# Gated-delta mixer of a two-layer hybrid network: residual normalised before the split, convolution from PSUM, heads inverted in fours

## The chip, the cores and the metric

The kernel runs on one core of one Trainium2 chip. The metric is the device time of one execution in microseconds (us). An execution consists of a span, in which the engines' instructions lie, and about 3 us around it.

## The reference, cut to what matters

The network has two layers of 1024 tokens by 1024 channels. Each layer is a mixer, a cross-attention to 256 memory tokens and a squared-ReLU MLP; before each of them stands a normalisation, `h = x * y * g`, where `y` is one over the root mean square of a token's channels and `g` a gain per channel. The change lies in the mixer of the second layer, a gated delta network:

```python
def c_mixer(h, w_in, conv_w, a_log, dt_bias, head_gain, w_out):
    qkv, gate, b, a = _split(h @ w_in, C_SIZES)      # 3072, 1024, 8 and 8 channels
    qkv = jax.nn.silu(short_conv(qkv, conv_w))       # four taps along the tokens, per channel
    q, k, v = _split(qkv, (GDN_QK, GDN_QK, GDN_VW))
    q = l2norm(q.reshape(B, T, GDN_HEADS, GDN_DK))   # 8 heads of 128
    k = l2norm(k.reshape(B, T, GDN_HEADS, GDN_DK))
    ...
    o = gated_deltanet(q, k, v, beta, log_alpha)
    o = rmsnorm(o, head_gain) * jax.nn.silu(gate...)
    return o @ w_out

def gated_deltanet(...):                             # chunks of 64 tokens
    lower = jnp.where(strict, beta * (k @ k.T) * decay, 0.0)
    sol = triangular_solve(lower + eye, rhs, ...)    # 64 x 64, for each head and chunk
    def step(S, inp):                                # over the 16 chunks of a head
        v_new = u - wk @ S
        o = qd @ S + att @ v_new
        S = S * jnp.exp(gl) + kd.T @ v_new
```

## The kernel before, in words

**Layout and order.** All of `x` lies transposed in SBUF, as 8 tiles of 128 channels by two halves of 512 tokens. The code runs under a scheduler with a timeline of its own: it decides in which order the instructions stand in each engine's queue, and each queue is then worked off strictly in that order. Instructions within `high_priority` are put ahead of others that are ready.

**Projections.** A projection of 128 output channels by one half of the tokens is 24 matmuls of 128x512 (`mm3`, L156 to L158): 8 blocks of input channels, with weights and `h` both split into a high and a low part (`hi*hi`, `lo*hi`, `hi*lo`). I call it a unit. ACT makes the high part of the weights (L149), POOL the low part (L150). The result lies in one of two PSUM banks of the tile `mm`. In program order the mixer has units 1 to 48 for the heads (six for each head: k, q and v of both halves), 49 to 64 for the output gates, then the memory's keys and values for the cross-attention, then 65 to 80 for the output projection.

**Start.** `mix_start` (L350) splits `x * g` into `hh` (ACT, L240) and `hl` (DVE, L241), 8 tiles for each half. The factor `y` isn't in it. Since it is a factor per token, it is multiplied on the result: `scaled` (L431, DVE) reads the bank, multiplies by the row `yy` and writes `raw` in SBUF. So the units can run before `y` is known.

**A head.** `gdn_head` (L958) projects k, q and v, with `scaled` as the eviction of each. `gdn_pre` (L987) then makes the convolution from `raw`: one ACT multiplication (L1002) and three DVE multiply-adds (L1004), a tanh (L1007, ACT) and a product (L1008, DVE), which together are the SiLU. It transposes (L1014, L1071), makes sums of squares (L1022) and the products of keys and queries (L1050), and multiplies them by decays `M`. `M` is loaded by a DMA from `gr` (L1037) and has one buffer; ACT makes `qe` of it (L1039). The triangles go through DRAM (`Ud`, `Bd`).

**Inversion.** `gdn_inv` (L1093) takes two heads at a time. It loads the 32x32 diagonal blocks of the triangles onto 64 partitions, solves them in 31 steps of two DVE instructions (L1109, L1114), stores them in `Xd`, loads the result as full tiles, transposes (L1124) and makes the 64x64 and 128x128 inverses of each head from five groups of 8 matmuls (L1129, L1136, L1140) with a subtraction or copy behind each group.

**Recurrence.** `gdn_rec` (L1145) walks over the 16 chunks of 2 heads, or at the end of 4, with `rec` matmuls (L1171 to L1191), each behind a DVE step (L1172, L1177, L1185). The order in the code is: heads 0 and 1, their inversion, their recurrence; the same for 2 and 3; heads 4 and 5 with inversion; heads 6 and 7 with inversion; the recurrence of heads 4 to 7.

**Gates.** `c_gate` (L871) projects, evicts with `scaled`, takes the tanh (L881) and the product (L882), and multiplies with the recurrence's output (`od`, L885).

Of the kernel before, what the change touches and what calls it, by code (L numbers as in the profile page):

```python
# [26 lines left out]
class Model:  # L27
# [216 lines left out]

    def split(self, vec, stat):
# [104 lines left out]
    def mix_start(self, l, bank, right):  # L350

        self.stat_bank = bank
        self.split(l, lambda half: self.y0 if l == 1 and half == 0 else self.rms_rows(half))
        self.flush()
        self.stat_bank = "sc"
        self.x_src = self.a["xT"]
        if l == 1:
            self.x_src = self.dr.tile([NK, 128, 1024], F32, name="x_scratch")
        self.x_close(self.x_src if l == 1 else None)
        self.open_right(right)  # L360
        self.direct = {}
        self.od = [self.dr.tile([128, 1024], F32, tag=f"od{l}{i}", name=self.nm("od")) for i in range(8)]

    def mix(self, l):
# [10 lines left out]
        else:  # L375
            with self.phase(
# [4 lines left out]
                self.mix_start(l, "o", dict(raw=5, kq=2, vc=1, M=1, qe=1, ua=1, kv=2))  # L381
# [437 lines left out]
    def mix_c(self):  # L819
# [4 lines left out]
        for pair in ((0, 1), (2, 3), (4, 5), (6, 7)):  # L824
            oq += [self.gdn_head(h) for h in pair]
            if pair[1] == 7:
                self.close_right()
                self.x_open(self.x_src, (0,))
                self.open_right(dict(B2=3, y2=3, S2=4))
            self.gdn_inv(pair)  # L830
            if pair[1] < 4:
                self.gdn_rec(pair, oq)
# [38 lines left out]
    def c_gate(self, h):  # L871
# [3 lines left out]
        def gate(i, w, half):  # L875
# [14 lines left out]
    def c_gates(self):  # L890
# [14 lines left out]
        for half in HALVES:  # L905
# [6 lines left out]
            self.scaled(rows[:32], ps[:32], half)  # L912
            nc.scalar.activation(rows[:32], rows[:32], AF.Identity, bias=bias)
# [44 lines left out]
    def gdn_head(self, h):  # L958

        nc = self.nc  # L960
        raw = {}

        def take(i, w, half):
            t = self.ph2("raw", [128, 515])
            ps = self.proj(w, half)
            with self.tc.high_priority():
                self.scaled(t[:, 3:515], ps, half)
                if half == 0:
                    nc.gpsimd.memset(t[:, 0:3], 0.0)
                else:  # L970
                    nc.gpsimd.tensor_copy(t[:, 0:3], raw[i, 0][:, 512:515])
            raw[i, half] = t
# [6 lines left out]
        for half in HALVES:  # L979
            self.gdn_pre(h, half, [raw[i, half] for i in (8 + h, h, 16 + h)], oq)  # L980
# [6 lines left out]
    def gdn_pre(self, h, half, raws, oq):  # L987
# [9 lines left out]
        kq = self.ph2("kq", [128, 2, 512])  # L997
        vc = self.keep("vc", dt=F32)
        for tl, raw, dst in zip((8 + h, h, 16 + h), raws, (kq[:, 0], kq[:, 1], vc)):
            cv = self.tmp()  # L1000
            wj = lambda j: self.convw[:, tl * 4 + j : tl * 4 + j + 1]
# [5 lines left out]
            nc.scalar.activation(dst, cv, AF.Tanh, scale=0.5)  # L1007
            nc.vector.scalar_tensor_tensor(out=dst, in0=dst, scalar=1.0, in1=cv, op0=ALU.add, op1=ALU.mult)  # L1008
# [762 lines left out]
```

## Time and profile before

| | us |
|---|---|
| three runs | 3225.93, 3229.2, 3229.65 (median 3229.2) |
| profiled execution | 3224.76 |
| its span | 3221.8 |
| PE (TensorE) busy | 3045.2 (95%) |
| DVE (VectorE) busy | 2115.9 (66%) |
| ACT (ScalarE) busy | 1330.2 (41%) |
| POOL (GpSimd) busy | 945.4 (29%) |

The second mixer lies between about 1495 and 2313 us of the span, from its first unit to the end of its output projection. A row of the timeline names the start and the length in us, the engine, the line, the operation, output and inputs; in brackets stands how long the engine was idle before it, and what it waited for. [...]

### The profile page before, as it was taken

How to read it: one execution, taken by the hardware profiler on the slowest of the kernel's cores; microseconds unless marked ns; L12 is line 12 of the kernel's file. 1: busy time of each engine (PE TensorE's matmuls, PEld its weight loads, DVE VectorE, ACT ScalarE, POOL GpSimd, SP SyncE). 2: the span in 40 equal slices, each digit the busy share in tenths (PEclk: the TensorE clock that was granted, in tenths of full speed). 3: DMA queues.
4: the chain of work that ended last, by engine and by line, in shares of the span. 5: the costliest groups of instructions: out<-in, count | busy, mean ns of one | idle time of the engine just before them, and what ended most of it. 6: DMA issues, size and time to landing. Idle time of an engine off the chain costs nothing.

```text
span 3221.8 us, 39997 instructions
## 1 busy us (share of the span) xinstructions
PE 3045.2 (95%) x14447; PEld 2511.5 (78%) x14447; DVE 2115.9 (66%) x3342; ACT 1330.2 (41%) x2525; POOL 945.4 (29%) x725
## 2 busy tenths in 40 slices
PE   8999989999899999998988899899999899999997
PEld 6777777888678878887777788788888678878886
DVE  5567475545786667777777775654454786667777
ACT  3254464424354454433443333234333354444442
POOL 2354565313000032234343333125323100023323
PEclk9999989999899999999999899999999999999998
DMA  4333553213244464443345556665212234474432
GB/s 151 109 119 103 156 175 119 70 39 102 75 143 157 152 238 167 147 164 100 87 117 142 149 156 187 191 231 187 66 56 77 97 111 149 157 250 173 148 144 79
DMA packets 268374, 438.04 MB, mean 136 GB/s; under 512 B 38064, under 2 KB 146832, under 8 KB 261008
## 3 DMA queue, kind: packets, MB, share of 16 engines
q1 hardware_dynamic: 268176, 435.50, 41.4%
q8 instruction: 113, 1.85, 0.2%
q14 instruction: 85, 0.70, 0.1%
HBM read 300.60 MB, written 134.81 MB: 135 GB/s over the span
## 4 chain that ended last, share of the span: by engine, by line
PE 33%; DVE 9%; DMA 4%; issue 4%; POOL 1%; ACT 1%; SPq 0%; POOLq 0%; DVEq 0%; ACTq 0%
PE mm L158 3%; PE mm L157 3%; PE mm L156 3%; PE ga L1453 2%; PE ga L1454 2%; PE ga L1455 2%; PE gb L1454 1%; DVE t L1004 1%; PE gb L1455 1%; PE gb L1453 1%; PE gc L1454 1%; PE gc L1455 1%; PE gc L1453 1%; PE mm L1454 1%; PE mm L1455 1%
## 5 line engine op out<-in xcount | busy, mean ns | idle before, releaser
L156 PE MATMUL mm<-hh,wh 128*128 128x512 f32 x1248 | 503.4, 404 | 8.2 <-DVE raw L431 3.5
L157 PE MATMUL mm<-hl,wh 128*128 128x512 f32 x1248 | 504.3, 404 | 0.0
L158 PE MATMUL mm<-hh,wl 128*128 128x512 f32 x1248 | 501.9, 402 | 0.0
L150 POOL TENSOR_TENSOR wl<-wr,wh 128x1024 fp32r<-128x1024 f32 x128 | 320.6, 2506 | 448.8 <-ACT wh L149 423.4
L1445 POOL TENSOR_TENSOR r<-r,r 128x512 f32<-128x512 f32 x64 | 92.0, 1458 | 881.8 <-DVE lo L1412 881.8
L1412 DVE TENSOR_TENSOR lo<-r,hi 128x1024 fp32r<-128x1024 f32 x192 | 252.8, 1317 | 133.1 <-ACT hi L1411 132.3
L1411 ACT CAST hi<-r 128x1024 fp32r<-128x1024 f32 x192 | 201.6, 1051 | 313.7 <-PE mm L1454 126.6
L156 PEld LDWEIGHTS mm<-hh,wh 128*128 128x128 f32 x1248 | 239.4, 192 | 59.2 <-DVE raw L431 4.8
L158 PEld LDWEIGHTS mm<-hh,wl 128*128 128x128 f32 x1248 | 240.5, 193 | 48.3 <-issue 0.9
L157 PEld LDWEIGHTS mm<-hl,wh 128*128 128x128 f32 x1248 | 240.2, 192 | 48.0 <-DVE hl L474 0.4
L149 ACT CAST wh<-wr 128x1024 fp32r<-128x1024 f32 x128 | 133.8, 1046 | 213.2 <-PE mm L157 120.8
L1412 DVE TENSOR_TENSOR lo<-br,hi 128x512 fp32r<-128x512 f32 x224 | 187.0, 852 | 32.9 <-ACT hi L1411 32.8
L1453 PE MATMUL ga<-hi,hi 128*128 128x512 f32 x528 | 206.7, 392 | 1.8 <-ACT w L1550 1.0
L1455 PE MATMUL ga<-hi,lo 128*128 128x512 f32 x528 | 206.5, 391 | 0.0
L1454 PE MATMUL ga<-lo,hi 128*128 128x512 f32 x528 | 206.5, 391 | 0.0
L1411 ACT CAST hi<-br 128x512 fp32r<-128x512 f32 x224 | 133.4, 619 | 152.0 <-PE ga L1455 90.0
L1454 PE MATMUL gb<-lo,hi 128*128 128x512 f32 x432 | 169.8, 393 | 7.6 <-DVE lo L1412 7.6
L1453 PE MATMUL gb<-hi,hi 128*128 128x512 f32 x432 | 169.8, 394 | 3.6 <-ACT hi L1411 3.1
L1454 PE MATMUL gc<-lo,hi 128*128 128x512 f32 x432 | 169.1, 391 | 2.3 <-DVE lo L1412 2.3
L1455 PE MATMUL gb<-hi,lo 128*128 128x512 f32 x432 | 169.0, 392 | 0.0
L1455 PE MATMUL gc<-hi,lo 128*128 128x512 f32 x432 | 168.2, 390 | 0.0
L1453 PE MATMUL gc<-hi,hi 128*128 128x512 f32 x432 | 167.8, 390 | 0.0
(515 smaller groups left out, 7228.5 us busy)
## 6 DMA issues: line engine op xcount, KB each, us to landing
r<-in_w SPq DMA_DIRECT2D x128, 512.0 KB, 4.2
br<-hd SPq DMA_DIRECT2D x56, 1024.0 KB, 5.4
hd<-w SPq DMA_DIRECT2D x160, 256.0 KB, 3.1
B<-Bd SPq DMA_DIRECT2D x64, 384.0 KB, 4.5
hd<-t SPq DMA_DIRECT2D x64, 256.0 KB, 5.2
wr<-in_c_w SPq DMA_DIRECT2D x32, 512.0 KB, 4.3
wr<-in_ab_w SPq DMA_DIRECT2D x24, 512.0 KB, 3.6
pj<-p SPq DMA_DIRECT2D x48, 256.0 KB, 2.1
```

The costliest lines, as they stand in the source:

```text
L149: nc.scalar.copy(hi, raw)
L150: (eng or nc.gpsimd).tensor_sub(lo, raw, hi.bitcast(F32))
L156: mm(out, w[0], x[0], start=first, stop=False)
L157: mm(out, w[0], x[1], start=False, stop=False)
L158: return mm(out, w[1], x[0], start=False, stop=last)
L1004: nc.vector.scalar_tensor_tensor(out=cv, in0=raw[:, j : j + 512], scalar=wj(j), in1=cv, op0=ALU.mult, op1=ALU.add)
L1411: nc.scalar.copy(hi, src)
L1412: (eng or nc.vector).tensor_sub(lo, src, hi.bitcast(F32))
L1445: self.nc.gpsimd.tensor_add(out[:, i : i + 512], a[:, i : i + 512], b[:, i : i + 512])
L1453: mm(ps, hi, b[k][0], start=first and k == 0, stop=False, skip_group_check=True)
L1454: mm(ps, hi, b[k][1], start=False, stop=False, skip_group_check=True)
L1455: mm(ps, lo, b[k][0], start=False, stop=last and k == 3, skip_group_check=True)
```

## The change

The first layer is as before. In the second mixer five things are different:

1. `split_normed` makes `t = x * g * y` (DVE), `hh` (a copy by ACT) and `hl = t - hh` (DVE): two DVE instructions for each tile in place of one. The second half needs its `y` first. `scaled` isn't used in this mixer any more.
2. The convolution reads the bank itself: one ACT multiplication and three DVE multiply-adds on `cv`. The first half's last three columns are kept by a small ACT copy, and the second half has three multiply-adds of one to three columns with them. `raw`, its three-column POOL copies and memsets are gone; `vc` has two buffers.
3. `c_gate` takes tanh and product from the bank.
4. `gdn_inv` takes four heads on 128 partitions: two rounds of the 31 steps in place of four.
5. Heads are taken in fours. The recurrences of heads 0 and 1 and of heads 2 and 3 both follow the first inversion.

```diff
+    def split_normed(self, vec, half, y):
+        for k in range(NK):
+            t = self.tmp()
+            nc.vector.scalar_tensor_tensor(
+                out=t, in0=self.x[k][half], scalar=self.gain(vec, k), in1=y, op0=ALU.mult, op1=ALU.mult
+            )
...
+            nc.scalar.copy(hi, t)
+            nc.vector.tensor_sub(lo, t, hi.bitcast(F32))
@@ mix_start
-        self.split(l, lambda half: self.y0 if l == 1 and half == 0 else self.rms_rows(half))
-        self.flush()
...
+            self.split_normed(l, 0, self.y0)
+            self.split_normed(l, 1, self.rms_rows(1))
@@ mix
-                self.mix_start(l, "o", dict(raw=5, kq=2, vc=1, M=1, qe=1, ua=1, kv=2))
+                self.mix_start(l, "o", dict(cv=3, kq=2, vc=2, M=1, qe=1, ua=1, kv=2))
@@ mix_c
-        for pair in ((0, 1), (2, 3), (4, 5), (6, 7)):
-            oq += [self.gdn_head(h) for h in pair]
+        for four in ((0, 1, 2, 3), (4, 5, 6, 7)):
+            oq += [self.gdn_head(h) for h in four]
...
-            self.gdn_inv(pair)
-            if pair[1] < 4:
-                self.gdn_rec(pair, oq)
+            self.gdn_inv(four)
+            if four[0] == 0:
+                self.gdn_rec((0, 1), oq)
+                self.gdn_rec((2, 3), oq)
@@ c_gate
-                self.scaled(t, ps, half)
-            nc.scalar.activation(e, t, AF.Tanh, scale=0.5)
-            nc.vector.scalar_tensor_tensor(out=t, in0=e, scalar=1.0, in1=t, op0=ALU.add, op1=ALU.mult)
+                nc.scalar.activation(e, ps, AF.Tanh, scale=0.5)
+                nc.vector.scalar_tensor_tensor(out=t, in0=e, scalar=1.0, in1=ps, op0=ALU.add, op1=ALU.mult)
@@ gdn_head, take
-            t = self.ph2("raw", [128, 515])
             ps = self.proj(w, half)
+            cv = self.keep("cv", dt=F32)
...
             with self.tc.high_priority():
-                self.scaled(t[:, 3:515], ps, half)
...
+                nc.scalar.mul(cv, ps, wj(3))
                 if half == 0:
...
+                    nc.scalar.copy(before[i][:, 0:3], ps[:, 509:512])
+                for j in (2, 1, 0):
+                    tap(j, ps[:, : 509 + j], 3 - j, 512)
+                if half == 1:
+                    for j in (2, 1, 0):
+                        tap(j, before[i][:, j:3], 0, 3 - j)
+            dst = (kq[half][:, 1], kq[half][:, 0], vc[half])[i // 8]
+            nc.scalar.activation(dst, cv, AF.Tanh, scale=0.5)
+            nc.vector.scalar_tensor_tensor(out=dst, in0=dst, scalar=1.0, in1=cv, op0=ALU.add, op1=ALU.mult)
@@ gdn_pre
-            cv = self.tmp()
-            nc.scalar.mul(cv, raw[:, 0:512], wj(0))
-            for j in range(1, 4):
-                nc.vector.scalar_tensor_tensor(
-                    out=cv, in0=raw[:, j : j + 512], scalar=wj(j), in1=cv, op0=ALU.mult, op1=ALU.add
-                )
```

The scheduler also puts the instructions in another order. In the following rows the second number behind a tile's name is its buffer; lines are those of each kernel by itself.

VectorE where the mixer starts, before: the splits `hl` of the second half, the first two evictions, and the sums of squares of the second half (L185, `yc` L199).

```order
L241 SCALAR_TENSOR_TENSOR hl_12935<-x_10470,gains,hh_12934 128x512
L241 SCALAR_TENSOR_TENSOR hl_12943<-x_10474,gains,hh_12942 128x512
L241 SCALAR_TENSOR_TENSOR hl_12939<-x_10472,gains,hh_12938 128x512
L185 TENSOR_TENSOR acc_12947<-acc_12947,t_12964 128x512
L431 SCALAR_TENSOR_TENSOR raw_13062<-mm_13063,yy_12818 128x512
L431 SCALAR_TENSOR_TENSOR raw_13090<-mm_13091,yy_12818 128x512
L185 TENSOR_TENSOR acc_12947<-acc_12947,t_12967 128x512
L199 TENSOR_SCALAR yc_12974<-o_12946 128x4
```

The first evictions stand ahead of the last of the second half's statistics.

VectorE at the same place, after: products `t` (L250) and `hl` (L256) of the second half, and the first convolution steps (L991), which read the banks of the first two units.

```order
L185 TENSOR_TENSOR acc_12931<-acc_12931,t_12951 128x512
L199 TENSOR_SCALAR yc_12958<-o_12930 128x4
L214 TENSOR_SCALAR t_12961<-ident,yc_12958 128x128 x4
L219 COPY yy_12970<-o_12930 128x512
...
L256 TENSOR_TENSOR hl_13005<-t_13002,hh_13004 128x512
L256 TENSOR_TENSOR hl_13011<-t_13008,hh_13010 128x512
L915 TENSOR_TENSOR wgc<-t_13207,wgc 128x8x16
L991 SCALAR_TENSOR_TENSOR cv_13123<-mm_13098,convw,cv_13123 128x511
L991 SCALAR_TENSOR_TENSOR cv_13157<-mm_13132,convw,cv_13157 128x511
L256 TENSOR_TENSOR hl_13017<-t_13014,hh_13016 128x512
```

Now the whole of the statistics and 15 of the 16 splits of the second half stand ahead of the first step that reads a bank.

ScalarE at the head pipeline (head 1), before: the convolution's multiplication reads `raw`.

```order
L1002 ACTIVATE t_14571<-raw_14388,convw 128x512
L1039 ACTIVATE qe_13753<-M_13751 128x512
L1002 ACTIVATE t_14578<-raw_14422,convw 128x512
L1017 ACTIVATE kv_13727,s_13719<-a_13722 128x128 x4
L1045 ACTIVATE M_13751<-M_13751,gd_ng 128x128 x4
```

ScalarE there, after: the multiplication (L996) reads `mm`, the bank itself; L1062 is the `qe` of before's L1039.

```order
L1006 ACTIVATE vc_13537<-cv_13685 128x512
L1062 ACTIVATE qe_13800<-M_13798 128x512
L149 CAST wh_13941<-wr_13939 128x1024
L996 ACTIVATE cv_13719<-mm_13694,convw 128x512
L1040 ACTIVATE kv_13774,s_13766<-a_13769 128x128 x4
L1068 ACTIVATE M_13798<-M_13798,gd_ng 128x128 x4
```

The first instruction that reads a finished bank now stands in a queue behind `qe`, which waits for `M`'s DMA; this repeats in nearly every half head.

TensorE in the last inversions, before (head 7, between its first and second group of products): 22 matmuls of a gate unit, of which the end stands here, lie ahead of the second group (L1136).

```order
L156 MATMUL mm_18429<-hh_12902,wh_18423 128x512
L157 MATMUL mm_18429<-hl_12903,wh_18423 128x512
L158 MATMUL mm_18429<-hh_12902,wl_18424 128x512
L156 MATMUL mm_18429<-hh_12906,wh_18423 128x512
L157 MATMUL mm_18429<-hl_12907,wh_18423 128x512
L1136 MATMUL i_17490<-zt_13034,Y_17474 128x64 x8
L1175 MATMUL a_17561<-B_3637_17559 128x128
```

TensorE in the last inversions, after (heads 5 and 6; L1152, L1159 and L1163 are before's L1129, L1136 and L1140, L1194 to L1214 its recurrence).

```order
L1163 MATMUL i_17194<-Y_17168,zt_13066 128x64 x8
L1194 MATMUL rec_15397<-S_15343,B_15395 128x128
L1203 MATMUL rec_15366<-y_15370,B_15364 128x128
L1152 MATMUL i_17204<-X_17167,Uk_17169 128x64 x8
L1198 MATMUL rec_15397<-B_15395 128x128
L1194 MATMUL rec_15413<-S_15373,B_15411 128x128
L1235 MATMUL o_15350<-ident,on_15248 128x128 x4
L1203 MATMUL rec_15397<-y_15401,B_15395 128x128
L1163 MATMUL i_17214<-Y_17168,zt_13067 128x64 x8
```

Between the groups of these heads stand steps of the recurrence of heads 2 and 3, and no projection.

## Rows read from the trace of the kernel before

**Rows 1.** Busy us (instructions) by engine in stretches; granted clock, DMA share, GB/s.

```profile
1640.00:1797.00 157.00, 137.93 (x680) 113.50 (x680) 128.97 (x262) 57.85 (x155) 53.56 (x45) 0.95 0.48 127
1797.00:1930.00 133.00, 119.49 (x673) 103.27 (x673) 100.66 (x236) 49.35 (x137) 41.08 (x35) 0.92 0.56 156
1930.00:2060.00 130.00, 119.45 (x677) 102.94 (x675) 84.96 (x187) 44.15 (x119) 35.48 (x25) 0.96 0.63 191
2060.00:2140.00 80.00, 73.73 (x424) 65.03 (x424) 32.89 (x63) 22.91 (x55) 13.60 (x8) 0.92 0.57 188
...
2230.00:2315.00 85.00, 85.00 (x380) 70.56 (x380) 29.42 (x39) 28.12 (x41) 25.82 (x12) 1.00 0.22 69
sum 825.00, PE 758.87 PEld 641.25 DVE 529.06 ACT 314.82 POOL 274.46; mean PE 94.86 PEld 80.16 DVE 66.13 ACT 39.35 POOL 34.31
```

**Rows 2.** PE's waits, 1480 to 2300 us: total us, times, longest.

```profile
PE i L1129 <- DMA X<-Xd: 10.2, 4, 3.2
...
PE mm L156 <- DVE raw L431: 3.5, 3, 3.0
```

**Rows 3.** DVE groups by line, 1490 to 2310 us: busy us, mean ns; idle before.

```profile
L1004 DVE SCALAR_TENSOR_TENSOR t<-raw,convw,t 128x512 f32<-128x512 f32 x144 | 122.1, 862 | 15.6 <-ACT t L1002 14.9
L1109 DVE TENSOR_TENSOR pr<-X,X 64x31 f32<-64x31 f32 (+15 forms) x124 | 55.7, 449 | 16.8 <-DMA X<-Ud 8.7 <-POOL X L1105 6.2
L1114 DVE TENSOR_TENSOR X<-X,pr 64x31 f32<-64x31 f32 (+15 forms) x124 | 48.4, 390 | 1.9
```

**Rows 4.** Single lines, same stretch: duration min/median/max in ns.

```profile
L1004 DVE SCALAR_TENSOR_TENSOR t<-raw,convw,t x144: 710/741/2887, 1551.8 to 1968.3; 128x512 f32<-128x512 f32 x144
...
L431 DVE SCALAR_TENSOR_TENSOR raw<-mm,yy x48: 651/677/692, 1514.3 to 1963.1; 128x512 f32<-128x512 f32 x48
```

**Rows 5.** Timeline, DVE and then PE at the mixer's start.

```profile
1501.36 0.69 DVE L219 COPY yy<-gc 128x512 f32<-128x512 f32 x1 [1.64 <-PE gc L215]
...
1514.27 1.28 DVE L431 SCALAR_TENSOR_TENSOR raw<-mm,yy 128x512 f32<-128x512 f32 x2
...
1525.44 0.69 DVE L219 COPY yy<-o 128x512 f32<-128x512 f32 x1 [0.53 <-PE o L215]
...
1515.01 0.50 PE L156 MATMUL mm<-hh,wh 128*128 128x512 f32 x1 [3.02 <-DVE raw L431]
...
1519.23 0.39 PE L158 MATMUL mm<-hh,wl 128*128 128x512 f32 x1
```

**Rows 6.** Timeline, the half head after 1607 us: SP's issue, then ACT.

```profile
1608.16 0.55 SPq L1037 DMA_DIRECT2D M<-gr  x1
...
1614.43 0.63 ACT L1039 ACTIVATE qe<-M 128x512 f32<-128x512 f32 x1 [4.18 <-DMA M<-gr]
1614.97 0.71 ACT L1002 ACTIVATE t<-raw,convw 128x512 f32<-128x512 f32 x1
```

**Rows 7.** Timeline of PE, marks between the stages.

```profile
1564.49 0.48 PE L156 MATMUL mm<-hh,wh 128*128 128x512 f32 x1
...
1814.54 0.40 PE L158 MATMUL mm<-hh,wl 128*128 128x512 f32 x1
...
2000.20 1.89 PE L1050 MATMUL a<-kq 128*128 128x256 f32 x8
...
2224.46 0.50 PE L156 MATMUL mm<-hh,wh 128*128 128x512 f32 x1 [1.14 <-ACT p L344]
```

**Rows 8.** Timeline of DVE: last 32x32 solve, and the inversions of heads 6 and 7.

```profile
2011.39 0.18 DVE L1109 TENSOR_TENSOR pr<-X,X 64x31 f32<-64x31 f32 x1 [2.99 <-DMA X<-Ud]
...
2060.46 1.25 DVE L1124 STREAM_TRANSPOSE Y<-X 128x1024 f32<-128x1024 f32 x1 [3.94 <-DMA X<-Xd]
...
2082.93 0.68 DVE L1141 TENSOR_TENSOR Y<-Y,i 128x512 f32<-128x512 f32 x1
...
2115.40 0.69 DVE L1141 TENSOR_TENSOR Y<-Y,i 128x512 f32<-128x512 f32 x1 [1.40 <-PE i L1140]
```

**Rows 9.** PE group by line, 1490 to 2310 us: one product of the inversion.

```profile
L1129 PE MATMUL i<-X,Uk 128*128 128x64 f32 x256 | 33.9, 284 | 12.7 <-DMA X<-Xd 10.2 <-DMA Uk<-Ud 2.5
```

More of the change, by code (lines that the diff above doesn't have):

```diff
@@ L243, in split_half @@
         self.y[half] = stat(half)
+    def split_normed(self, vec, half, y):
+        nc = self.nc
+        for k in range(NK):
[3 more added lines that the diff above has]
+            )
+            hi = self.res[half].tile([128, 512], F32R, tag=f"hh{k}{half}", name=self.nm("hh"))
+            lo = self.res[half].tile([128, 512], F32R, tag=f"hl{k}{half}", name=self.nm("hl"))
+            nc.scalar.copy(hi, t)
+            nc.vector.tensor_sub(lo, t, hi.bitcast(F32))
+            self.h[k][half] = (hi, lo)
     def split(self, vec, stat):
@@ L352, in mix_start @@
         self.stat_bank = bank
-        self.split(l, lambda half: self.y0 if l == 1 and half == 0 else self.rms_rows(half))
-        self.flush()
+        if l == 0:
+            self.split(l, self.rms_rows)
+            self.flush()
+        else:
+            self.h = [[None, None] for _ in range(NK)]
+            self.split_normed(l, 0, self.y0)
+            self.split_normed(l, 1, self.rms_rows(1))
         self.stat_bank = "sc"
@@ L823, in mix_c @@
         self.late = {}
-        for pair in ((0, 1), (2, 3), (4, 5), (6, 7)):
-            oq += [self.gdn_head(h) for h in pair]
-            if pair[1] == 7:
+        for four in ((0, 1, 2, 3), (4, 5, 6, 7)):
+            oq += [self.gdn_head(h) for h in four]
+            if four[0] == 4:
                 self.close_right()
@@ L911, in c_gates @@
             rows = self.tmp()
-            self.scaled(rows[:32], ps[:32], half)
-            nc.scalar.activation(rows[:32], rows[:32], AF.Identity, bias=bias)
+            nc.scalar.activation(rows[:32], ps[:32], AF.Identity, bias=bias)
             for i in range(4):
@@ L960, in gdn_head, with tap @@
         nc = self.nc
-        raw = {}
+        kq = [self.ph2("kq", [128, 2, 512]) for half in HALVES]
+        vc = [self.keep("vc", dt=F32) for half in HALVES]
+        before = {}
         def take(i, w, half):
-            t = self.ph2("raw", [128, 515])
             ps = self.proj(w, half)
+            cv = self.keep("cv", dt=F32)
+            wj = lambda j: self.convw[:, i * 4 + j : i * 4 + j + 1]
+            def tap(j, src, n0, n1):
+                nc.vector.scalar_tensor_tensor(
+                    out=cv[:, n0:n1], in0=src, scalar=wj(j), in1=cv[:, n0:n1], op0=ALU.mult, op1=ALU.add
+                )
             with self.tc.high_priority():
-                self.scaled(t[:, 3:515], ps, half)
+                nc.scalar.mul(cv, ps, wj(3))
                 if half == 0:
[L969 to L972, printed above, removed]
+                    before[i] = self.tp.tile([128, 4], F32, tag="H", name=self.nm("b"), bufs=6)
+                    nc.scalar.copy(before[i][:, 0:3], ps[:, 509:512])
[7 more added lines that the diff above has]
+            nc.vector.scalar_tensor_tensor(out=dst, in0=dst, scalar=1.0, in1=cv, op0=ALU.add, op1=ALU.mult)
             if (i, half) == (16, 0):
@@ L979, in gdn_head @@
         for half in HALVES:
-            self.gdn_pre(h, half, [raw[i, half] for i in (8 + h, h, 16 + h)], oq)
+            self.gdn_pre(h, half, kq[half], vc[half], oq)
         return oq
@@ L985, in ph2, with gdn_pre @@
         return pool.tile(list(shape), F32, tag=tag, name=self.nm(tag), bufs=self.bufs[tag])
-    def gdn_pre(self, h, half, raws, oq):
+    def gdn_pre(self, h, half, kq, vc, oq):
         nc = self.nc
@@ L996, in gdn_pre @@
         c4 = slice(4 * half, 4 * half + 4)
-        kq = self.ph2("kq", [128, 2, 512])
-        vc = self.keep("vc", dt=F32)
-        for tl, raw, dst in zip((8 + h, h, 16 + h), raws, (kq[:, 0], kq[:, 1], vc)):
-            cv = self.tmp()
-            wj = lambda j: self.convw[:, tl * 4 + j : tl * 4 + j + 1]
-            nc.scalar.mul(cv, raw[:, 0:512], wj(0))
-            for j in range(1, 4):
-                nc.vector.scalar_tensor_tensor(
-                    out=cv, in0=raw[:, j : j + 512], scalar=wj(j), in1=cv, op0=ALU.mult, op1=ALU.add
-                )
-            nc.scalar.activation(dst, cv, AF.Tanh, scale=0.5)
-            nc.vector.scalar_tensor_tensor(out=dst, in0=dst, scalar=1.0, in1=cv, op0=ALU.add, op1=ALU.mult)
         self.put(h, half, 0, kq[:, 0])
```

## Prediction

> **What bounds the kernel now.** I read the stretches first [rows 1]. Over the second mixer, 1490 to 2315 us, PE is busy 758.9 of 825 us, so it idles 66 us. The last row of it, the output projection, is the measure of a full pace: 380 matmuls in 85.0 us at clock 1.00, 0.224 us each, so a unit of 24 takes 5.4 us. In the four stretches from 1640 to 2140 the granted clock is 0.92 to 0.96; one minus it, times PE's busy time, is 7 + 10 + 5 + 6 = 28 us of clock lost. About 95 us, idle and clock together, is all that a change which leaves PE's work alone can win; the rest of it is matmuls that stay. DVE is full only in 1640 to 1797 (129.0 of 157); in 2060 to 2140 it is busy 32.9 of 80.
>
> Then I read what PE waits for [rows 2]. The first entry is the inversion's load `X<-Xd`, 10.2 us in 4; evictions hold PE for 3.5 us in all. So the engine that is relieved, DVE, is not what PE mostly waits for. It acts through chains: split, eviction, solve.
>
> **What the change takes from DVE and adds.** In [rows 3, 4]: `scaled` goes, 48 x 0.677 = 32.5 us, and 16 in the gates at the same price, 11. The solve's 55.7 + 48.4 = 104 us halve if an instruction's time goes by its free size and not by its partitions: -52; no row has 128 partitions, so 0 to -52, and I take -52, since steps as short as 0.18 us are used already at 64. The convolution's 144 steps have two SBUF operands, mean 862 ns but median 741; the eviction, which reads a bank and SBUF, never took over 692. Steps from the bank are bounded by 0.677 and 0.862; I take 0.68, the row with the new operands: -26. Added are 16 splits, 16 x 0.68 = 11, and 72 steps of a few columns, at the shortest step's 0.18 us: 13. The sum is 97 us less of DVE. ACT gets 24 copies of three columns; ACT is busy 314.8 of 825 us [rows 1], which covers them, and without that cover they cost some 0.2 us each in stage 2. Two `vc` buffers add no instruction.
>
> [...]
>
> I price the path in five stages, each with its own end on PE.
>
> **1. The start: +18 us (8 to 25).** Before, the first eviction starts at 1514.27, PE waits 3.02 us for it, and the third unit starts at 1515.01. [rows 5] After, the first convolution step stands behind the half-0 split, which needs the row `yy` copied at 1501.36, behind half 1's sums and behind 15 of half 1's 16 split instructions. From 1502: 16 x 0.69 = 11 for half 0, with 3 additions of the MLP and 7 sums between at 0.68 = 7, so 1520; then the row `yy` of half 1, by way of PE and POOL, for which I allow 5 us: 1525 (before it came at 1525.44, with PE busy ahead of it); then 15 x 0.6 to 0.69, up to 10: 1535. The banks of units 1 and 2 are held till then, so unit 3 starts about 1535, 20 us late. Units 3 to 8 had small waits before, for the gates' weights and `yy`, which this overlaps; on the other hand `M` of head 0 comes later. I carry 18 us: unit 9, which began at 1564.49 [rows 7], begins at 1582. Low end: the splits hide in the MLP's tail. High end: nothing overlaps.
>
> **2. Units 9 to 36: 213 us in place of 250.** Before they lie between 1564.49 and 1814.9 [rows 7] and contain the inversions of heads 0 and 1, ten products of 8 matmuls at about 0.216 us, the distance of their starts (their mean of 0.284 is a length), 1.73 us each [rows 9]: 17 us, which move out to stage 3. The floor for a head is 6 x 5.4 = 32.4 plus twice 3.6 for `gdn_pre` (the 1.89 us of the L1050 group and as much for transposes and sums): 39.6. To that I add the new wait. The multiplication that first reads a bank stands behind `qe` in ACT's queue, and `qe` waits for `M`: issued 1608.16, read 1614.43, with ACT idle 4.18 us [rows 6]. There the multiplication behind it, at 1614.97, read `raw` and held no bank. Now it does, for its own 0.7 and three steps of 0.68: about 3 us with hand-overs, of a unit's 5.4. A bank may thus be late by 2.4 us and cost nothing; ACT's wait of 4.2 exceeds that by about 2 us for each half head: 4 to 5.5 for a head, 43.5 to 45 in all. 28 units are 4.67 heads: 203 to 210, plus 8 where the first solve of four fills DVE and waits for its load. I take 213: unit 36 ends about 1795, 20 us earlier than before.
>
> **3. To the last `kk` (L1050 of head 7): 146 us.** PE's work there is 15 units = 81, five `gdn_pre` = 18, 20 products of the first inversion = 35: 134 at full clock. At 0.92, as the stretch from 1797 has [rows 1], 146: 1941, where before it began at 2000.20 [rows 7]. This is 59 us ahead, but part of the work before it has only moved behind it.
>
> **4. Last solve and inversion: 60 + 84 us.** From that `kk` the time to the transposed inverse was 2061.7 - 2002.1 = 60 us: load until 2011.39, 31 steps, store, load, transpose to 2061.7 [rows 8]. Four heads have the same number of steps: 60 again, till 2001. In it PE has the rest of unit 51, units 52 to 54 and a few recurrence steps, some 30 us of work: it starves for about 30 us, which is new. Then the inversions stand on PE one head behind the other. Head 6 alone took 2061.7 to 2083.6 = 22 us, head 7 with gate units between 32 [rows 8]. Four at 19 (half of the hops find their input ready) are 76; the store and load of the result add 8 (bounds 70 to 96 together). That is 2085. Beside them lie gate units and the recurrences of heads 0 to 3, which hide there.
>
> **5. To the output projection: 122 us.** Before, from the last inverse at 2116.1 [rows 8] to the output projection at 2224.46 [rows 7]: 108, with two to three gate units; after, with four more, 108 + 4 x 5.4 less the 7 us that PE idles before: 122. So 2207 in place of 2224.5, **-17 us**. Nothing behind it is changed.
>
> The profiled execution took 3224.8, which gives 3207; the median is 4.4 above it. **Predicted: 3211.**
>
> **Rivals.**
>
> *PE freed.* DVE loses a fifth of its work in the mixer, evictions and solves come at once, and half of the 95 us is won: 3229 - 48 = 3181. For it: DVE is full in 1640 to 1797, the clock is at 0.95 there, and `X<-Xd` leads PE's waits. Against it: evictions cost 3.5 us now. It holds if ACT reaches the bank within 2.4 us.
>
> *Nothing moves.* The start's 18 to 25 us, the starved 30 and the late inversions eat the gain of stage 2: stage 4 at 96 and the start at 25 give 3211 + 12 + 7 = 3230.
>
> *Slower: banks held behind `qe`.* Place: units 9 to 48. If `M` comes later than I reckon, so that PE waits for all of 4.2 us in each half head, the granted clock falls too. [...] It decides from the point at which ACT's idle time before `qe` grows past 4 us after a bank is full. For it: PE then has no third bank. Against it: in the timeline ACT's wait is under 5 us. [...]
>
> *The relief isn't there.* If a step on 128 partitions takes twice as long and steps from the bank are as long as before, DVE is where it was and the start is left: 3229 + 18 - 10 = 3237. I count it to the slower side.
>
> **How the numbers follow.** Forecast, 3195 to 3222: 0.41. PE freed, 3165 to 3195: 0.16. Nothing moves: 0.20. Slower, both cases together, 3236 to 3262: 0.23. A measurement can tell 0.2%, 6.5 us, from no change. Of the forecast's range all lies below 3222.7. So faster 0.57, same 0.20, slower 0.23. The forecast alone has 3195 to 3222; for 8 in 10 the range goes to 3170, which leaves out some 0.03, and up to 3247, which leaves out some 0.12.
>
> **What would show it.** Stage 1: unit 3 on PE starts near 1535, unit 9 near 1582. Stage 2: PE's waits have entries for the bank behind ACT's `cv`, each 1 to 3 us, and ACT still idles for `qe`; if these are absent, PE is freed. Convolution steps at 0.68 us, solve steps at 0.4 on 128 partitions. Stage 4: PE's busy share falls under 0.7 between the last `kk` and the first late inversion. What would make it wrong: a start that costs 5 us, or a scheduler order that, on the chip, lets PE run through stage 4 with gate units.

## The result and the profile after

The changed kernel took 3259.6 us (median of 4 runs, 3255.7 to 3262.5) against 3229.4 for the kernel before: 1.0092 times as long, 95% interval 1.0077 to 1.0106, so **30 us slower**. I had forecast 3211, 18 us faster. Its profiled execution took 3262.5, with a span of 3260.8.

The busy time of the engines by stretch, columns as in [rows 1]; the last line is the whole of the mixer up to its end at 2350:

```profile
1490.00:1545.00 55.00, 36.76 (x163) 27.19 (x161) 39.90 (x73) 22.12 (x38) 5.25 (x4) 0.81 0.29 89
1640.00:1797.00 157.00, 134.44 (x611) 109.78 (x612) 107.63 (x223) 63.84 (x176) 52.34 (x30) 0.96 0.40 110
1930.00:2060.00 130.00, 118.68 (x680) 104.43 (x678) 67.52 (x175) 38.88 (x118) 26.56 (x18) 0.87 0.63 190
2060.00:2140.00 80.00, 74.04 (x459) 65.75 (x460) 25.74 (x69) 20.61 (x57) 11.21 (x10) 0.89 0.58 185
...
1490.00:2350.00 860.00, 770.82 (x4040) 650.85 (x4039) 466.89 (x976) 319.03 (x811) 251.61 (x149) 0.93 0.49 145
```

DVE did get less work: 467 us in the mixer against 529 [rows 1]; in 1640 to 1797, where it was busy 129 us, it is busy 108. PE idles 860 - 771 = 89 us, where it idled 66; and the granted clock, which was 0.96 in 1930 to 2060, is 0.87 there. What PE waits for has changed too (columns as in [rows 2]):

```profile
PE mm L156 <- DVE cv L991: 41.6, 15, 14.8
PE mm L156 <- DVE s L1046: 6.2, 3, 2.5
PE rec L1203 <- DVE y L1200: 5.1, 3, 2.4
```

The inversion's load `X<-Xd`, which led the list before with 10.2 us, is gone from the top; in its place stand 41.6 us for `cv`, the convolution that holds a bank. 14.8 of it is one wait at the start; the other 26.8 lie in 14 waits.

The marks on PE that answer to [rows 7] (start of unit 37, last product of keys, output projection), and from DVE the two that answer to [rows 8]:

```profile
1812.59 0.47 PE L156 MATMUL mm<-hh,wh 128*128 128x512 f32 x1 [1.55 <-DVE cv L991]
...
1960.88 1.89 PE L1073 MATMUL a<-kq 128*128 128x256 f32 x8
...
2254.75 0.50 PE L156 MATMUL mm<-hh,wh 128*128 128x512 f32 x1
...
2016.81 1.25 DVE L1147 STREAM_TRANSPOSE Y<-X 128x1024 f32<-128x1024 f32 x1 [0.69 <-DMA X<-Xd]
...
2114.34 0.69 DVE L1164 TENSOR_TENSOR Y<-Y,i 128x512 f32<-128x512 f32 x1
```

The output projection starts 30 us late (2254.8 against 2224.5), which is the whole of the median's difference. (The spans of the two profiled executions differ by 39 us; the other 9 lie behind that mark, where the code is the same.) The kernel after is 39 us ahead of the one before at the last product of keys (1960.9 against 2000.2) and level at the last inverse (2115.0 against 2116.1). So it loses its lead between these two marks, and 31 us more behind them.

### The profile page after: what moved, and what is told of

It reads as the page before. It is cut to its first block, busy times and chain, and to the rows that moved or that the text cites. A ratio compares the mean times of both kernels' runs of the same rounds, so it can differ in the third digit from the quotient of the medians.

```text
span 3260.8 us, 39882 instructions
## 1 busy us (share of the span) xinstructions
PE 3055.2 (94%) x14447; PEld 2521.2 (77%) x14447; DVE 2040.9 (63%) x3240; ACT 1329.2 (41%) x2549; POOL 920.7 (28%) x673
## 5 line engine op out<-in xcount | busy, mean ns | idle before, releaser
L156 PE MATMUL mm<-hh,wh 128*128 128x512 f32 x1248 | 506.8, 406 | 49.5 <-DVE cv L991 41.6
L150 POOL TENSOR_TENSOR wl<-wr,wh 128x1024 fp32r<-128x1024 f32 x128 | 312.2, 2440 | 538.5 <-ACT wh L149 486.2
L157 PEld LDWEIGHTS mm<-hl,wh 128*128 128x128 f32 x1248 | 240.2, 192 | 47.4 <-DVE hl L493 0.4
L1477 PE MATMUL mm<-lo,hi 128*128 128x512 f32 x400 | 160.1, 400 | 9.5 <-DVE lo L1435 9.5
```

The costliest lines, as they stand in the source:

```text
L150: (eng or nc.gpsimd).tensor_sub(lo, raw, hi.bitcast(F32))
L156: mm(out, w[0], x[0], start=first, stop=False)
L157: mm(out, w[0], x[1], start=False, stop=False)
L1477: mm(ps, hi, b[k][1], start=False, stop=False, skip_group_check=True)
```

## The experiments

Each kernel is compared with the kernel before, run on the same chip beside it; the ratio is given with its 95% interval, and I turn it into us with 3229.

### One part at a time

**norm_only** makes only the first part of the change.

```diff
@@ mix_start
-        self.split(l, lambda half: self.y0 if l == 1 and half == 0 else self.rms_rows(half))
-        self.flush()
...
+            self.split_normed(l, 0, self.y0)
+            self.split_normed(l, 1, self.rms_rows(1))
+            self.y = None
...
@@ scaled
+        if self.y is None:
+            return self.nc.vector.tensor_copy(t, ps)
```

> The kernel before, with only the first part of the change: x * g * y is split, half 1 after its statistics, and the eviction into raw is a plain DVE copy in place of the product with y; convolution, solve and order are those of before. Theory S (the start costs: the first banks wait for half 1's statistics and split) expects 15 to 20 us more than before, with PE waiting about 10 us or more for its third unit and the lower clock behind that. Theory B (the loss comes from banks held by the convolution) expects this kernel within 6 us of before.

Measured: 1.0005 (0.9991 to 1.0019), 2 us. The stall at the start is there, on PE:

```profile
1527.16 0.80 PE L156 MATMUL mm<-hh,wh 128*128 128x512 f32 x1 [10.55 <-DVE raw L451]
1527.75 0.63 PE L157 MATMUL mm<-hl,wh 128*128 128x512 f32 x1
```

PE waits 10.55 us for the first bank and comes back at a lower clock: the granted clock is 0.62 in the next 4 us, and a matmul lasts 0.63 us there with starts 0.43 us apart, where the output projection of the kernel before, at clock 1.00 [rows 1], has medians of 0.39 and 0.227. Unit 9 starts at 1572.5, 8 us late, but the last product of keys at 2000.6, where before had 2000.2. So theory S falls: this delay at the start isn't a delay of the end. My reading is that PE works the lag off because later in the mixer it waits for chains and not for projections; that reason was not tested by itself.

**pairs_back** takes the changed kernel and undoes the fours; it has parts 1 to 3.

```diff
-        for four in ((0, 1, 2, 3), (4, 5, 6, 7)):
+        for pair in ((0, 1), (2, 3), (4, 5), (6, 7)):
...
```

> The changed kernel with heads solved in pairs again, in the order of before. Theory L expects it 12 to 20 us faster than the changed kernel, so 10 to 18 us slower than before. If the late inversions are not the loss, it is as slow as the changed kernel (30 us over before) or slower, since DVE has 52 us of solve more.

Measured: 1.0053 (1.0034 to 1.0071), 17 us (14 by the medians), as theory L had it. Against norm_only that is some 15 us for the convolution and the gates from the bank together.

**fours_only** takes the kernel before and makes only parts 4 and 5.

```diff
-        for pair in ((0, 1), (2, 3), (4, 5), (6, 7)):
+        for four in ((0, 1, 2, 3), (4, 5, 6, 7)):
...
```

> The kernel before, with only heads solved and taken four at a time, and the recurrences of heads 0 to 3 behind that. Theory L (four late inversions in a row leave PE without cover) expects 12 to 20 us more than before, with the granted clock under 0.9 between 1980 and 2100 us. If the 52 us that DVE saves in the solve are worth something and L is wrong, it is 5 to 15 us faster than before.

Measured: 1.0079 (1.0052 to 1.0105), 25 us slower, although the solve is halved; theory L had the direction, but 12 to 20. The granted clock in 1980 to 2100 is 0.83, and 0.93 before. So both parts lose, the fours more; 2, 15 and 25 sum to 42, and the change as a whole lost 30. They overlap.

### Why the bank costs time

In the changed kernel one release reads like this, on ACT and then on DVE and PE. The unit whose bank is at stake (the seventh) ended near 1572:

```profile
1574.74 0.63 ACT L1062 ACTIVATE qe<-M 128x512 f32<-128x512 f32 x1 [5.36 <-DMA M<-gr]
1575.27 0.62 ACT L1006 ACTIVATE vc<-cv 128x512 f32<-128x512 f32 x1
1578.52 1.19 ACT L1054 ACTIVATE kv<-a,s 128x128 f32<-128x128 f32 x4 [2.63 <-DVE s L1052]
1579.60 1.27 ACT L1068 ACTIVATE M<-M,gd_ng 128x128 f32<-128x128 f32 x4
1580.77 0.68 ACT L996 ACTIVATE cv<-mm,convw 128x512 f32<-128x512 f32 x1
...
1581.53 0.75 DVE L991 SCALAR_TENSOR_TENSOR cv<-mm,convw,cv 128x511 f32<-128x511 f32 x1 [1.33 <-ACT b L999]
1582.20 0.87 DVE L1081 SCALAR_TENSOR_TENSOR ua<-a,s,M 128x256 f32<-128x256 f32 x2
1582.98 1.52 DVE L991 SCALAR_TENSOR_TENSOR cv<-mm,convw,cv 128x510 f32<-128x510 f32 x2
...
1584.65 0.47 PE L156 MATMUL mm<-hh,wh 128*128 128x512 f32 x1 [0.87 <-DVE cv L991]
```

The bank is full at 1572, but ACT stands at `qe` till 1574.7, then waits for a statistic of the head (2.63 us), and reaches the bank at 1580.8, nearly 9 us late. Three steps on DVE, with other work between them, free it at 1584.5, and unit 9 starts at 1584.65. PE shows only 0.87 us of idle time for the bank. It had idled 2.77 us before, at 1579.8, for ACT's `kv`, which stands in the same queue ahead of `cv`; the rest of the lag lies in between, in unit 8 and work of the head. Four kernels ask what holds the bank.

**m_two_buffers** changes one number of the changed kernel.

```diff
-                self.mix_start(l, "o", dict(cv=3, kq=2, vc=2, M=1, qe=1, ua=1, kv=2))
+                self.mix_start(l, "o", dict(cv=3, kq=2, vc=2, M=2, qe=1, ua=1, kv=2))
```

> The changed kernel with two buffers for M in place of one, so that the load of M can be issued a half head earlier and ACT does not wait for it ahead of the next convolution. Theory B in the form 'banks are held because ACT's queue stands at qe' expects ACT's idle time before qe to fall from 88 us to under 30, PE's waits for cv in units 7 to 48 from 27 us to under 10, and the time to fall by 15 to 25 us, to 5 to 15 us over before. If the banks are held by the order of DVE's and ACT's work itself, or if L and S are all of the loss, it stays within 6 us of the changed kernel.

Measured: 1.0097 (1.0073 to 1.0121), as slow as the changed kernel. But it didn't test what it was meant to: ACT still idled 71.0 us before `qe` (88.1 in the changed kernel), 52.1 of it for `M`'s load. The free buffer didn't move the load: SP's queue still issued it right behind the stores of `ua` (in one half head the stores at 1609.2 and 1609.6, the load at 1610.7). PE's waits for `cv` behind the start did fall, from 26.8 to 17.4 us, and the time didn't.

**pairs_m_early** puts the load ahead of the head's projections in the code, in pairs_back, and gives `M` two buffers.

```diff
+        self.early = {(h, half): self.load_m(h, half) for half in HALVES} if h else {}
         ...
-        M = self.keep("M", dt=F32)
+        M = self.early.pop((h, half)) if (h, half) in self.early else self.load_m(h, half)
         ...
-        nc.sync.dma_start(out=m3, in_=self.gr[c4, h].partition_broadcast(128))
```

> The changed kernel with heads in pairs, and M in two buffers whose load is issued at the head of gdn_head, ahead of the head's projections (from head 1 on), so that M has landed long before qe. Theory B1 (a bank is held because ACT's queue stands at qe waiting for M) expects ACT's idle time before qe under 15 us, PE's waits for cv behind the start under 8 us, and the 14 us that pairs_back has over before to fall to 0 to 5. Theory B2 (the bank is held by the length and the place of the convolution itself: four instructions on two engines, with statistics of the head between) expects it within 5 us of pairs_back.

Measured: 1.0019 (1.0008 to 1.0030), 6 us, so 11 less than pairs_back. Again not by the way I meant: the scheduler left most of the loads where they were (14 of the 16 are used 5.6 to 7.8 us after their issue), and ACT waits 53.6 us for `M` (68.1 in pairs_back). The order around it changed, and PE's waits for `cv` between 1535 and 2000 us fell from 22.9 to 16.4. I don't count this run for or against `qe` as the cause.

**pairs_dve_mul** takes ACT out of the release.

```diff
-                nc.scalar.mul(cv, ps, wj(3))
+                nc.vector.tensor_scalar_mul(cv, ps, wj(3))
```

> The changed kernel with heads in pairs, and the first multiplication of the convolution on DVE in place of ACT, so that a bank's release does not pass ACT's queue except for the copy of three columns in the first half. B1 expects second-half banks to be released in 3 to 4 us after the unit, and 5 to 10 us off pairs_back. B2, with 33 us more on DVE, expects no gain or up to 10 us more than pairs_back.

Measured: 1.0017 (1.0004 to 1.0030), 5 us in place of 17, in B1's direction and somewhat more than its 5 to 10, although DVE has 35 us more to do (48 multiplications of 739 ns).

**pairs_copy_first** keeps the convolution where pairs_back has it, but from a copy.

```diff
             with self.tc.high_priority():
+                raw = self.keep("raw", dt=F32)
+                nc.vector.tensor_copy(raw, ps)
+                ps = raw
+            if True:
                 nc.scalar.mul(cv, ps, wj(3))
```

> pairs_back with the bank copied into SBUF by one DVE instruction first, and the same convolution from that copy, in the same place. Theory B (the bank is held through the convolution) expects PE's waits for evictions behind the start under 5 us, units 9 to 36 about 10 us shorter, and 0 to 6 us over before in place of 14. If the place of the convolution or the gates from the bank cost the 12 us, it is 10 to 18 over before.

Measured: 1.0018 (1.0003 to 1.0032), 6 us. PE's waits between 1535 and 2000 us, the first `cv` or eviction entry of pairs_back and of pairs_dve_mul, and the first entry of all in pairs_copy_first, where no eviction appears among the first:

```profile
PE mm L156 <- DVE cv L990: 22.9, 13, 7.0
```

```profile
PE mm L156 <- DVE cv L990: 9.8, 8, 3.2
```

```profile
PE a L1076 <- DVE s L1049: 16.9, 3, 6.6
```

Copied first, the 22.9 us of waits for evictions are gone, though 16.9 us for a statistic on DVE stand in their place; with the multiplication on DVE 9.8 are left. From the start of unit 9 to the start of unit 37, pairs_back takes 265 us, pairs_copy_first 250 and pairs_dve_mul 242. So the stretch with the heads gets shorter when the bank is freed sooner, as theory B had it, and both kernels lose 5 to 6 us in place of 17. As much goes when the multiplication leaves ACT's queue as when the bank is copied, so ACT's queue seems to be the larger part of the hold. That `qe` alone is the reason was not shown; the statistic behind it delays as well.

That the hold is the cause of the 11 us at the end is likely, but a rival is left. pairs_m_early starts unit 37 as late as pairs_back does (at 1851.9 and 1845.1; 1828.8 and 1829.9 in the two kernels that free the bank), and it too loses only 6 us. Another order of the instructions can thus win the same without the units' coming earlier.

### Why the fours cost time

**last_four** and **first_four** split the fours, on the kernel before.

```diff
-        for pair in ((0, 1), (2, 3), (4, 5), (6, 7)):
+        for g in ((0, 1), (2, 3), (4, 5, 6, 7)):      # last_four
+        for g in ((0, 1, 2, 3), (4, 5), (6, 7)):      # first_four
```

> The kernel before with heads 4 to 7 solved and taken as four, heads 0 to 3 in pairs as before. L1 expects +15 to +23 us against before, nearly all of fours_only's 23, and PE's idle and lower-clock time between the last product of keys and the last inverse. L2 expects -5 to +5.

> The kernel before with heads 0 to 3 solved and taken as four, heads 4 to 7 in pairs as before. Theory L1 (the loss of fours_only comes from the second four, whose inversions stand late and one behind the other) expects -10 to +4 us against before. Theory L2 (it comes from the first four: the recurrences of heads 0 to 3 and with them the gates of these heads are delayed) expects +15 us or more.

Measured: last_four 1.0047 (1.0029 to 1.0064), 15 us, as L1 had it; first_four 1.0114 (1.0092 to 1.0136), 37 us, against L1 and as L2 had it. Neither is the whole. The first four alone is even worse than both together; why, no run shows. PE's granted clock in 1930 to 2060 is 0.79 in first_four. What is missing there shows in the count of the product `Y` by `vb` of the recurrence (L1175 of before), before and after the last product of keys. Stretches with PE and PEld busy, clock, DMA; the kernel before, then the changed one:

```profile
1480.00:2000.20 520.20, 10.18 (x48) 8.33 (x48) 0.94 0.49 137
2000.20:2230.00 229.80, 17.13 (x82) 13.21 (x80) 0.96 0.68 217
```

```profile
1480.00:1960.88 480.88, 2.91 (x14) 2.19 (x14) 0.94 0.44 124
1960.88:2260.00 299.12, 24.68 (x114) 20.10 (x114) 0.90 0.64 205
```

A step of a head by a chunk has two records of this line. The kernel's chunks have 128 tokens, so that a head has 8 steps (not 16, the number of the reference's chunks, which I gave for the recurrence above), and all heads 64. Before, 24 steps were done when the heads' projections ended; after, 7. The other 17 steps of the recurrence have moved behind, where only the gates' units are left to stand beside them. Is that the order of the heads in the code, or the joined solve?

**order_only** has the order of the fours, but solves each four as two pairs.

```diff
+        for four in ((0, 1, 2, 3), (4, 5, 6, 7)):
...
+            self.gdn_inv(four[:2])
+            self.gdn_inv(four[2:])
```

> The kernel before with the heads, inversions and recurrences in the order of the fours, but each four solved as two pairs, so no DVE work is saved. If the loss of fours_only (23 us) is in the order (the recurrences of heads 0 to 3 all behind the last head's projections), this kernel is 20 to 35 us slower than before and has at the last product of keys about 50 to 70 of 592 recurrence products done, where before has 214. If the loss is in the solve of four itself (later first result, longer load), it is within 8 us of before.

Measured: 0.9990 (0.9978 to 1.0002), no loss. The first transposed inverse on DVE in the kernel before, in fours_only and in order_only:

```profile
1733.37 1.25 DVE L1124 STREAM_TRANSPOSE Y<-X 128x1024 f32<-128x1024 f32 x1 [5.45 <-DMA X<-Xd]
```

```profile
1817.17 1.25 DVE L1125 STREAM_TRANSPOSE Y<-X 128x1024 f32<-128x1024 f32 x1 [3.69 <-DMA X<-Xd]
```

```profile
1732.17 1.25 DVE L1126 STREAM_TRANSPOSE Y<-X 128x1024 f32<-128x1024 f32 x1 [0.17 <-DMA X<-Xd]
```

The count of `Y` by `vb` up to the last product of keys, in fours_only and in order_only:

```profile
1480.00:1942.00 462.00, 2.53 (x12) 1.81 (x12) 0.95 0.46 127
1480.00:1965.50 485.50, 7.53 (x36) 5.96 (x36) 0.96 0.48 133
```

That is 6 steps with the joined solve, and 18 with the same order in the code and two pairs. A joined solve can't start before the triangles of its fourth head are there. In fours_only the first inverse comes 84 us later than before, and all of the recurrence of heads 0 to 3 with it. In order_only the scheduler starts the first pair's solve as soon as heads 0 and 1 are done, whatever the code's order, and there is no loss. So it is the solve of four itself: it halves DVE's work (57 us for 104 in the changed kernel) and takes nothing off the latency, which is one solve in either case (from its first step to that inverse 74.5 us before, from 1658.84, and 78.3 in fours_only, from 1738.87), while the first head waits for the fourth.

**Cover.** If those late recurrences cost because nothing stands beside them, projections that depend on nothing should help. The gates of heads 4 to 7 don't read a recurrence's output (L885 is for heads 0 to 3).

```diff
-        for h in range(8):
+        for h in (4, 5, 6, 7, 0, 1, 2, 3):
             self.c_gate(h)
```

> fours_only with one line more: the gates of heads 4 to 7 are projected ahead of those of heads 0 to 3. These eight units wait for no recurrence, so they can stand beside the recurrences of heads 0 to 3 and the second solve. Theory L2 in the form 'recurrences without projections beside them' expects the granted clock between 1930 and 2060 us to rise from 0.88 to 0.94 or more and the 23 us over before to fall to 5 to 12. If the length of the chain (recurrence behind recurrence, inversion behind inversion) sets the end whatever stands beside it, it stays within 6 us of fours_only.

> The kernel before with the same one line (gates of heads 4 to 7 first), as a control: its recurrences of heads 0 to 3 lie beside head projections already, so L2 expects -5 to +3 us against before. If the order of gates helps in any case, by 10 us or more here, it says nothing on the fours.

> The changed kernel with the same one line. L2 expects 10 to 18 us off the 30 us that the changed kernel has over before; the chain theory expects 24 to 34 over before.

> after_gates_late with the convolution's first multiplication on DVE, as in pairs_dve_mul, where that took 8 of 14 us. If both losses (banks behind ACT's queue; recurrences without cover) are independent, it is 3 to 10 us faster than after_gates_late. If the banks' loss is absorbed by the later stretch, as the unit marks of the changed kernel against fours_only suggest, it is within 4 us of it.

> pairs_back with the gates of heads 4 to 7 first. If the banks' 12 us and the gates' 21 us are independent, it is 4 to 12 us faster than before. If a later stretch takes up the banks' loss, it is 15 to 24 faster, like before_gates_late.

> order_only with the gates of heads 4 to 7 first; it differs from fours_gates_late (8 us faster than before) in nothing but the solve, two pairs in place of four together. If the joined solve's late first result is the loss, it is 16 to 28 us faster than before, like before_gates_late. If saved DVE time counts once the gates stand beside, it is 0 to 8 faster, no better than fours_gates_late.

| kernel | without | gates of heads 4 to 7 first |
|---|---|---|
| before | 1 | 0.9933 (0.9908 to 0.9958) |
| order_only | 0.9990 | 0.9933 (0.9917 to 0.9949) |
| fours_only | 1.0079 | 0.9975 (0.9962 to 0.9988) |
| pairs_back | 1.0053 | 1.0009 (0.9994 to 1.0023) |
| changed kernel | 1.0092 | 1.0015 (0.9999 to 1.0031) |
| changed, multiplication on DVE | not run | 1.0031 (1.0017 to 1.0044) |

PE and the clock from 1930 to 2060 us in fours_only and, with the gates turned round, in fours_gates_late:

```profile
1930.00:2060.00 130.00, 114.20 (x676) 101.27 (x675) 64.86 (x167) 34.68 (x103) 24.89 (x17) 0.88 0.60 182
```

```profile
1930.00:2060.00 130.00, 126.54 (x755) 110.81 (x755) 75.35 (x167) 36.67 (x98) 29.23 (x18) 0.99 0.62 188
```

With units to stand beside the recurrences, PE goes from 114 to 127 us busy and from 0.88 to 0.99 of the clock, and the fours gain 34 us, more than I had expected. But the control gains 22 too, where I had expected nothing; by my own words the turn of the gates then says nothing on the fours alone. The kernel before lacked such units too: in the control PE is busy 126.4 of the 130 us from 1930, before 119.5 [rows 1]. If the gains add, 34 - 22 = 12 us belong to the fours. What does tell is the comparison of fours_gates_late and order_gates_late, which differ in the solve alone: 14 us (0.9975 and 0.9933, with intervals that do not meet). My expectation for order_gates_late by the late first result was met: 22 us faster than before.

The changed kernel gains 25 us by the turn, where L2 had 10 to 18. after_dve_mul_gates is no faster than after_gates_late, if anything slower. With the fours, the banks' loss seems to be taken up later, as the second of its two expectations had it. pairs_gates_late, on the other hand, gains 14 us only and not 22; it is 3 us over before, and neither of its expectations was met. How banks and gates act on each other there stays open.

**before_gates_late** and **order_gates_late** are the fastest kernels here, 22 us (0.67%) faster than the kernel before and 52 faster than the changed one. They contain nothing, or only the order of the heads, of the change.

## Why the prediction was wrong

By its own stages, the changed kernel's marks against the forecast's:

| stage | forecast, us | measured, us | off |
|---|---|---|---|
| 1, start of unit 9 late by | 18 | 20 (1584.7) | +2 |
| 2, units 9 to 36 | 213 | 228 (to 1812.6) | +15 |
| 3, to the last product of keys | 146 | 148 (1960.9) | +2 |
| 4a, solve, to the transposed inverse | 60 | 57 (2018.1) | -3 |
| 4b, four inversions | 84 | 97 (2115.0) | +13 |
| 5, to the output projection | 122 | 140 (2254.8) | +18 |

**Stages 4 and 5, the wrong step.** The forecast says that the recurrences of heads 0 to 3 "hide there", beside the late inversions, and takes stage 5 as before's 108 us plus four gate units less 7 us of idle time. It never counted how much of the recurrence before had done by that point. It is 24 steps against 7, which the count above shows. At about five products for each step, 0.22 us apart (starts at 2075.47 and 2075.69 in the kernel before), some 17 x 5 x 0.22 = 19 us of PE's work (an estimate) went into a stretch that I had priced without it. Most of it went into stage 4: between the last product of keys and the last inverse 29 steps ran, where before had 15; behind it, 28 against 26. And nothing hides there, since in stage 4b PE itself is the engine that is full: busy 91.6 of the 97 us, at a granted clock of 0.86. Nor does PE starve in stage 4a. It is busy 47.4 of 57.2 us, a share of 0.83 where my sign was under 0.7, because the recurrences fill it. In stage 5 the gate units are about as forecast (6, and before 2.6), but PE idles 12.7 us (before 8.8), where I had taken 7 off, and the clock is 0.94 (before 0.97).

The recurrence is also work that waits: 5.1 us of PE's waits are for its `y` on DVE alone, and the clock from the last product of keys to the output projection is 0.90, before 0.96. The leads that I counted as gain (59 us at the last product of keys, 39 measured) were to that extent work not yet done. fours_only, with 25 us lost and a lead of 58 us at the same point, shows the same without the other parts.

**Stage 2, a term mis-sized.** The mechanism stood in the forecast, and as a rival: banks held behind ACT's queue. I took 2 us of wait for a half head from `qe` alone. The trace shows ACT at the bank up to 9 us late, since behind `qe` stands a second wait, for a statistic. And the steps from the bank took 742 ns each, not 680: I had taken the price of a two-operand eviction for them. The upper end of the range for the slower side, 3262, is near the measured time, but that is luck: pairs_back, which has these banks, lost 17 us, and the rest came from the fours, which the forecast had on the side of gain. The granted clock did fall behind a wait at the start, to 0.60 from 1515.0 to 1519.3 in the kernel before and to 0.50 from 1529.0 to 1533.0 in the changed one. But where the rival put it, it did not fall: from the start of unit 9 to that of unit 37 it is 0.96 in the changed kernel, and 0.95 before. So the range from 3236 to 3262 was an estimate of mine, and that clock is lost in each half head was not shown. pairs_copy_first, which copies the bank out, lost 6 us in place of 17.

**Stage 1, right in size and wrong in effect.** The start's delay was 20 us at unit 9, and 14.8 of it is one wait, on PE:

```profile
1529.04 0.77 PE L156 MATMUL mm<-hh,wh 128*128 128x512 f32 x1 [14.80 <-DVE cv L991]
```

But norm_only shows that 8 us at unit 9 (1572.5 there against 1564.5) leave 2 at the end, and pairs_dve_mul, whose unit 9 starts at 1588.0, is 5 us over before in all. Adding the stages assumed that one path runs through all of them. A delay of projections was worth little here, which fits a chain of solves and recurrences that ends last behind them.

**What held.** DVE's relief was about as forecast in the solve (57 us for 104, in 31 + 31 steps of two):

```profile
L991 DVE SCALAR_TENSOR_TENSOR cv<-mm,convw,cv 128x511 f32<-128x511 f32 (+1 forms) x144 | 106.6, 742 | 69.3 <-ACT b L999 36.5 <-ACT cv L996 31.5
L991 DVE SCALAR_TENSOR_TENSOR cv<-b,convw,cv 128x1 f32<-128x1 f32 (+2 forms) x72 | 35.6, 494 | 0.0
L1137 DVE TENSOR_TENSOR X<-X,pr 128x31 f32<-128x31 f32 (+15 forms) x62 | 30.5, 492 | 1.0
...
L1132 DVE TENSOR_TENSOR pr<-X,X 128x31 f32<-128x31 f32 (+15 forms) x62 | 26.5, 428 | 2.7 <-DMA X<-Ud 1.7
```

The convolution gave 122 - 107 = 15 us in place of 26, and its small steps took 36 in place of 13. By the medians a step costs the same from the bank (743 ns) as from SBUF (741), not 0.06 us less, as I took. What went away are 15 of the 144 old steps that took 1.0 to 2.9 us, each of them while a POOL instruction ran; together they lay 17.5 us above the median. None of this relief shows in the time: PE's waits for DVE were for the place of its instructions and not for their amount. That DVE isn't what PE mostly waits for stood in the first part of the forecast, and I should have given more weight to it.

## What to carry to other kernels

Joining the solves of four heads in one instruction saved DVE's time (57 us for 104 in the changed kernel) and made the first head wait for the last (its inverse came 84 us later in fours_only). Where work is joined so, count, at a fixed mark of the program, how much dependent work was done before and is done after, and price the difference where it goes. A lead at such a mark is a gain only if nothing was left behind. The instruction that reads a PSUM bank held that bank here for all that stood ahead of it in its engine's queue, up to 9 us; the kernel that copies the bank out first, by one DVE instruction, lost 6 us in place of 17.

## What the runs showed of the hardware

An instruction of the solve took on 128 partitions nearly what it took on 64: the subtraction of a step 376 ns in the median on 128 (L1137), and 352 on 64 partitions (L1114 of before), with the same free sizes.

Some very small instructions were long. The 72 steps of one to three columns, the only ones of the convolution with two operands in SBUF, took from 0.18 to 1.77 us:

```profile
L991 DVE SCALAR_TENSOR_TENSOR cv<-mm,convw,cv x144: 702/743/752, 1524.9 to 1937.6; 128x511 f32<-128x511 f32 x48, 128x510 f32<-128x510 f32 x48, 128x509 f32<-128x509 f32 x48
L991 DVE SCALAR_TENSOR_TENSOR cv<-b,convw,cv x72: 184/209/1773, 1555.5 to 1938.3; 128x1 f32<-128x1 f32 x24, 128x2 f32<-128x2 f32 x24, 128x3 f32<-128x3 f32 x24
```

The first of them, and POOL beside it:

```profile
1555.55 1.21 DVE L991 SCALAR_TENSOR_TENSOR cv<-b,convw,cv 128x1 f32<-128x1 f32 x1
...
1554.35 2.39 POOL L150 TENSOR_TENSOR wl<-wr,wh 128x1024 fp32r<-128x1024 f32 x1 [41.90 <-ACT wh L149]
```

The step on one column lasts till 1556.76, and POOL's instruction, which reads two tiles of SBUF, till 1556.74. 22 of the 72 small steps took over 0.4 us, and each of them ended within 0.03 us of the end of a POOL instruction that reads SBUF (L150, L1063 or L1065); the 144 steps with one operand in the bank stayed within 702 to 752 ns, though 45 of them ran beside such an instruction. These small steps stand between the large ones (the one above between those that start at 1554.88 and 1556.68), so they lengthen the hold of the second half's banks.
